# Heads' stage of a hybrid attention and SSD backbone: tensor products in written order, and fewer transfers on the SP queue

## The chip, the cores and the metric

The kernel runs on one core of one Trainium2 chip. The metric is the device time of one execution in microseconds (us). The kernel before takes 2391.28 us, the median of three runs (2390.47 to 2392.25).

## What is computed

Two layers run over 512 latent tokens and 256 context tokens, width 1024, all in float32. The part of a layer that the change touches, cut from the reference:

```python
h  = rmsnorm(x_lat, norm1_w[l]) * (1.0 + sc1) + sh1          # hc the same for context
q, k, v, z, xbc, dtf, dtb = split_proj(h @ w_in)             # 4 heads of 2x64, v 128 wide
q = apply_rope(rmsnorm(q, q_norm_w)); k = apply_rope(rmsnorm(k, k_norm_w))
s = einsum("bqhid,bkhid->bhiqk", q, k_all) * HEAD_DIM ** -0.5
p = softmax(s); w = p[:, :, 0] - lam * p[:, :, 1]            # differential attention
attn = rmsnorm(w @ v_all, subln_w) * (1.0 - lam_init)
ssd  = gated_group_rmsnorm(ssd_bidirectional(...) + d_res * xs, z, ssd_norm_w)
x_lat = x_lat + g1 * (concat([attn, ssd]) @ w_out)
h2 = rmsnorm(x_lat, norm2_w[l]) * (1.0 + sc2) + sh2
x_lat = x_lat + g2 * expert_choice_ffn(h2, ...)              # 16 experts, SwiGLU, top 64 tokens each
```

The context stream is updated in layer 0 only. The vectors `sh`, `sc`, `g` come from `silu(c) @ w_mod`, six blocks of 1024 columns.

## The kernel before

Each layer has four stages: the SSD projections and chunk states, the heads' stage, the output stage, and the experts. Tokens lie in tiles of 128 (four latent, two context). A float32 product is made of three fp32r products (`mm3`, L179): high by high, high by low, low by high part.

In the heads' stage each of four heads projects each of six tiles: `Head.proj` runs eight steps of three products into `pacc` and yields after each step, so a tile has 24 products. Beside these run pieces, each a Python generator: `rope` (norm and rotation, then four transposes `qtr`, L1793), `attend` of the head before (score products `sc` L1828, maximum `nm` L1832, exponentials `e` L1837, weight transposes `wtr` L1855, output products `po` L1860), the last SSD chunks (`yd` L1098, `yo` L1103, `Y` L1139) and the modulation (`macc` L335, from weights `mr` in 512 KB pieces, seven buffers). The score tile `sc` has one buffer in PSUM.

`Slots.tick` advances every piece by one step and draws on the generator of products between them. A tile has two ticks of four steps, so 12 products per tick. The order in which instructions stand on an engine is not the written one: a scheduler orders all engines by its own estimate of when operands are ready, and the engines then run in that fixed order.

In the output stage `op_in` (L1193) loads a tile `mixin` of the concatenated heads, scales it (L1204), transposes it (`mtr`, L1210), and `oacc` products with `w_out` follow; `x_load` brings the residual, and the new `x1` is stored. For layer 0 also the normalised `xn` is stored in `xn2d`, from which the experts gather.

The kernel's loads and stores go through `ld` (L162) and `st` (L169), which issue on the queue of SyncE (SP), in order; a few small loads at the start go through `lds` on GpSimd (POOL). A weight block is loaded as `raw` (four buffers), rounded to its high part on ScalarE (L131) and its low part is made on POOL (L143) or VectorE (L145). The expert weights `gw` are loaded by SP too, in pairs (gate and up, 704 KB each).

Of the kernel before, what the change touches and what calls it, by code (L numbers as in the profile page):

```python
# [18 lines left out]
P = 128  # L19
D = 1024  # L20
# [56 lines left out]
class Slots:  # L77
# [7 lines left out]
    def add(self, *gens):  # L85
        self.live += [[g, None] for g in gens]

    def tick(self, fill=None, n=0, each=0):
        turn, done, first = sorted(self.live, key=lambda x: x[1] is None), 0, True
        while turn:  # L90
            again = []
            for i, x in enumerate(turn):
                x[1] = next(x[0], self)
                if x[1] is STEP:
                    again.append(x)
                while first and not each and done < (n - 1) * (i + 1) // len(turn):
                    next(fill, None)
                    done += 1
            for _ in range(min(each, n - 1 - done)):
                next(fill, None)  # L100
                done += 1
            turn, first = again, False
        while done < n:
            next(fill, None)
            done += 1
        self.live = [x for x in self.live if x[1] is not self]
# [43 lines left out]
class Net:  # L150
# [16 lines left out]

    def st(self, o, i):
        return self.nc.sync.dma_start(o, i)  # L169

    def split(self, hi, lo, x, sub=None):

# [261 lines left out]
    def mixer(self, l):  # L434
        nc, tc, psp = self.nc, self.tc, self.psp
# [10 lines left out]
        q = Slots()  # L446

        if l == 0:
            with tc.manual_schedule(engines=ENGINES):
                mp = open_("mp")  # L450
                self.first(pre)
                f = self.mods_first(pre, mp)
# [70 lines left out]
        first, ssd = [], []  # L523
# [52 lines left out]
        for i, t in enumerate(tiles):  # L576
            f = self.z_proj(l, t, wz, psp, q)
# [13 lines left out]
        self.att1 = open_("at")  # L591
        q.add(self.rope_tables(l, self.att1))
        wo = []
        for h in range(4):
            if h == 1:
                self.attB = open_("atB")
            st = hd[h + 1].stage(W) if h < 3 else None
            hd[h].open()
            for i, t in enumerate(SEQ):
                f = hd[h].proj(t, q)  # L600
                if i == 5 and st:
                    f = paired(f, st)
                for half in range(2):
                    tk = 2 * i + half
                    if ssd and over(ssd):
                        ssd = None
                        zp.release()
                        ch.release()
                        s1.release()
                        com.release()  # L610
                        self.scp.release()
                        self.scp = self.scores(l)
                        mo = open_("mo", "right")
                        mr = lambda: mo.tile([P, 1024], F32, tag="mr", name="mr", bufs=7)
                        q.add(itertools.chain(*([self.mods(0, range(2, 6), mo, mr)] if l == 0 else [self.mods(1, (2, 3, 4), mo, mr)])))
                    if h > 0 and tk in (5, 7, 9, 11):
                        q.add(hd[h - 1].attend(tk // 2 - 2))
                    if l == 0 and h > 0 and tk in (1, 3):
                        q.add(hd[h - 1].attend(NL + tk // 2))
                    q.tick(f, 4)  # L620
                if i % 2:
                    q.add(hd[h].rope(t - 1))
            for _ in st or ():
                pass
        mo.release()
        hp.release()
        self.xnp = open_("xn", "right") if l else None
# [16 lines left out]
        for i, t in enumerate(tiles):  # L644
# [6 lines left out]
            for j in range(nt):  # L651
# [25 lines left out]
                else:  # L677
                    n = 4
# [462 lines left out]
    def z_out(self, l, t, ap):  # L1141

        nc, y = self.nc, self.Y[:, t]
        for g in range(2):
            junk = ap.tile([P, 256], BF16, tag="yj", name="yj", bufs=1)
            nc.scalar.activation(junk, y[:, 256 * g:256 * g + 256], AF.Square, scale=1.0 / 16, accum_out=self.mss[:, t, g:g + 1])
        self.st(self.mixd[l][t * P:(t + 1) * P, 512:1024], y)
        yield


# [32 lines left out]

    def g1_load(self, l, s, op):
        self.G1 = op.tile([P, D], F32, tag="G1", name="G1")
        self.ld(self.G1, self.modd[l, s:s + 1, 2 * D:3 * D].to_broadcast([P, D]))

    def x_load(self, l, t, op):
        self.xs[t] = op.tile([P, D], F32, tag="xr", name="xr", bufs=1)
        self.ld(self.xs[t], self.xsrc(l, t))  # L1190

    def op_in(self, l, t, op, psp):

        nc = self.nc
        mx = op.tile([P, D], F32, tag="mixin", name="mixin", bufs=1)
        n = 4 if t >= NL else 3
        self.ld(mx[:, 512:D], self.mixd[l][t * P:(t + 1) * P, 512:D])
        self.ld(mx[:, 0:n * P], self.mixd[l][t * P:(t + 1) * P, 0:n * P])
        self.mT[t] = mT = [op.tile([P, KD, P], F32, tag=f"mT{j}", name="mT", bufs=2) for j in range(2)]
        rs = yield from self.rsqrt_steps(op, self.mss[:, t, 0:n + 2], n + 2, 1.0, f"mrs{n}")  # L1200
        yield
# [75 lines left out]
    def op_half(self, l, t, b, op, psp):  # L1277
# [14 lines left out]
        if b == 0:  # L1292
            return
        s = int(t >= NL)
        self.st(self.rows_of(l, t), x1)
        yield STEP
        ss = op.tile([P, 1], F32, tag="ss3", name="ss3", bufs=2)
        nc.vector.tensor_tensor(ss, self.ss2[t][:, 0:1], self.ss2[t][:, 1:2], op=OP.add)
# [15 lines left out]
        if l == 0:  # L1314

            xn = self.xn[t]
            nc.vector.tensor_scalar(xn, x1, rs, None, op0=OP.mult)
            self.st(self.xn2d[t * P:(t + 1) * P], xn)
        else:
            nc.vector.tensor_copy(self.rms[:, t:t + 1], rs)  # L1320
        nc.vector.reciprocal(sm, sm)
# [384 lines left out]
class Head:  # L1706
# [107 lines left out]
    def attend(self, t):  # L1814
# [53 lines left out]
        if own:  # L1868
# [4 lines left out]
            nc.tensor.transpose(tr, ob, n.ident)  # L1873
            yield from n.head_split(*([m[:, t] for m in n.oT] if n.oT else [m[:, 3] for m in n.mT[t]]), tr)
            return
        n.st(n.mixd[self.l][t * P:(t + 1) * P, P * self.h:P * self.h + P], ob)


# [41 lines left out]
```

## Time and profile before

| | us |
|---|---|
| median of three runs | 2391.28 |
| the profiled execution | 2389.74 |
| its span in the trace | 2388.0 |
| TensorE (PE) busy | 2176.3 (91%) |
| VectorE (DVE) busy | 931.7 (39%) |
| ScalarE (ACT) busy | 652.2 (27%) |
| GpSimd (POOL) busy | 433.5 (18%) |

The profiled execution is 1.54 us under the median, and 1.74 us of it lie outside the span. A wait is time in which an engine stood still, put down to the instruction that released it last. Products overlap on PE, so the time from one start to the next says what one costs, not its own duration. SPq, ACTq and POOLq are the issuing queues of these engines.

### The profile page before, as it was taken

What the parts mean: (1) busy time and instruction counts of PE and PEld (TensorE: products, weight loads), DVE (VectorE), ACT (ScalarE), POOL (GpSimd) and SP (SyncE); (2) the same over time, 40 slices, a digit from 0 to 9 for tenths busy, and PEclk for the clock granted to TensorE, in tenths of its full rate; (3) what the DMA queues carried; (4) which work ended last, traced back from release to release, by engine and by line L of the source; (5) the groups of instructions that cost most, each with busy time, mean ns of one, the idle gap of its engine ahead of it and who ended that gap; (6) DMA issues with size and microseconds to landing.
All of it is one profiled execution on the core that took longest, in us unless ns stands there. A gap on an engine that the chain in (4) does not pass through costs nothing. (4 is left out here: it accounts for less than half of the span.)

```text
span 2388.0 us, 49731 instructions
## 1 busy us (share of the span) xinstructions
PE 2176.3 (91%) x20620; PEld 1247.0 (52%) x20620; DVE 931.7 (39%) x2586; ACT 652.2 (27%) x1791; POOL 433.5 (18%) x554
## 2 busy tenths in 40 slices
PE   6898998999999999999987988989799999988776
PEld 4677788685444444444435667877543333232322
DVE  5787578772111111111116786786611110101010
ACT  4434477532111111111113334575101010101000
POOL 4464342000101001001003464341000000000000
PEclk9999999999999999999998999999899999999999
DMA  7323723589999999999994226334999999999997
GB/s 250 91 78 102 266 72 107 186 285 344 390 407 401 398 405 393 401 400 400 395 390 127 86 66 198 112 109 139 347 400 416 385 416 410 416 411 415 412 413 314
DMA packets 229790, 701.69 MB, mean 294 GB/s; under 512 B 30340, under 2 KB 79324, under 8 KB 229564
## 3 DMA queue, kind: packets, MB, share of 16 engines
q1 hardware_dynamic: 220076, 681.37, 73.9%
q0 software_dynamic: 9488, 17.14, 3.5%
q8 instruction: 163, 2.67, 0.4%
q14 instruction: 63, 0.52, 0.1%
HBM read 674.66 MB, written 23.76 MB: 292 GB/s over the span
## 5 line engine op out<-in xcount | busy, mean ns | idle before, releaser
L1518 PE MATMUL gl<-gw,xeT 128*32 128x512 f32 (+1 forms) x8192 | 654.8, 466 | 61.9 <-DMA gw<-w_up 59.1
L1518 PEld LDWEIGHTS gl<-gw,xeT 128*32 128x32 f32 x8192 | 279.1, 111 | 441.4 <-issue 396.5
L1559 DVE SCALAR_TENSOR_TENSOR th<-th,gl 128x256 f32<-128x256 f32 (+1 forms) x96 | 37.5, 391 | 698.5 <-ACT th L1558 698.4
L1572 PE MATMUL yl<-rt,hl 128*32 128x512 f32 x2040 | 257.7, 595 | 9.5 <-PE gl L1518 9.2
L1558 ACT ACTIVATE th<-gl 128x256 f32<-128x256 f32 (+1 forms) x96 | 35.1, 366 | 768.1 <-PE gl L1518 761.4
L179 PE MATMUL pacc<-rt,H 128*128 128x384 f32 (+1 forms) x768 | 203.1, 346 | 7.1 <-POOL rt L143 2.4
L1699 DVE SCALAR_TENSOR_TENSOR ys<-yl,gate,G2l 128x512 f32<-128x512 f32 x32 | 24.0, 751 | 380.5 <-PE yl L1572 367.4
L1609 PE MATMUL gc<-gw,xeT 128*32 128x352 f32 x2048 | 171.2, 459 | 0.0
L1700 POOL DMA_INDIRECT out<-ys,sidx x16 | 24.8, 1549 | 730.6 <-DVE ys L1699 589.8
L179 PEld LDWEIGHTS pacc<-rt,H 128*128 128x128 f32 x768 | 134.1, 192 | 19.8 <-issue 6.0
L1572 PEld LDWEIGHTS yl<-rt,hl 128*32 128x32 f32 x2040 | 70.4, 109 | 141.3 <-issue 83.2
L179 PE MATMUL xacc<-H,rt 128*128 128x512 f32 (+1 forms) x448 | 135.9, 381 | 7.0 <-ACT H L816 6.6
L1456 POOL DMA_INDIRECT xe<-xn2d,gidx x16 | 15.1, 943 | 617.6 <-PE xet L1466 507.0
L179 PE MATMUL pacc<-rt,L 128*128 128x384 f32 (+1 forms) x384 | 127.1, 331 | 0.0
L1471 ACT ACTIVATE xeT<-xet,MC,A 128x64 f32<-128x64 f32 (+1 forms) x256 | 74.1, 426 | 178.5 <-PE xet L1466 178.5
L143 POOL TENSOR_TENSOR rt<-raw,rt 128x384 fp32r<-128x384 f32 (+1 forms) x88 | 101.5, 1176 | 80.7 <-ACT rt L131 66.4
L179 PE MATMUL oacc<-woh,mT 128*128 128x512 f32 x304 | 107.4, 411 | 0.0
L1572 PE MATMUL yl<-wd,hl 128*32 128x512 f32 x776 | 102.2, 599 | 2.2 <-DMA wd<-w_down 1.7
L1609 PEld LDWEIGHTS gc<-gw,xeT 128*32 128x32 f32 x2048 | 68.8, 110 | 56.6 <-issue 44.8
L179 PEld LDWEIGHTS xacc<-H,rt 128*128 128x128 f32 x448 | 83.1, 199 | 22.9 <-ACT H L816 7.4
L179 PE MATMUL xacc<-L,rt 128*128 128x512 f32 (+1 forms) x224 | 82.6, 371 | 3.0 <-POOL L L879 2.1
L1485 PE MATMUL xpk<-x,one 128*64 128x512 f32 x256 | 81.8, 633 | 3.4 <-DVE one L1481 3.4
(410 smaller groups left out, 3279.0 us busy)
## 6 DMA issues: line engine op xcount, KB each, us to landing
gw<-w_gate SPq DMA_DIRECT2D x256, 704.0 KB
gw<-w_up SPq DMA_DIRECT2D x256, 704.0 KB
rt<-w_down SPq DMA_DIRECT2D x255, 512.0 KB
wd<-w_down SPq DMA_DIRECT2D x97, 512.0 KB
mr<-w_mod SPq DMA_DIRECT2D x80, 512.0 KB
raw<-w_in SPq DMA_DIRECT2D x48, 256.0 KB
raw<-w_in SPq DMA_DIRECT2D x64, 192.0 KB
RB<-acsd SPq DMA_DIRECT2D x20, 512.0 KB
```

Of the source, the lines that this page charges most:

```text
L143: e.tensor_tensor(lo.bitcast(F32R), x, hi, op=OP.subtract)
L179: self.nc.tensor.matmul(o, a[x].bitcast(F32R), b[y].bitcast(F32R), start=start and i == 0, stop=stop and i == 2, **kw)
L1456: self.nc.gpsimd.indirect_dma_start(out=xe[0:n], out_offset=None, in_=self.xn2d[0:rows], in_offset=bass.IndirectOffsetOnAxis(ap=idx[0:n, e ...
L1471: nc.scalar.activation(xT[:, kk, c:d], tr[:, k, c - a:d - a], AF.Identity, scale=self.A2[:, s, kk:kk + 1], bias=self.MC[:, l, s, 24 + kk:2 ...
L1485: nc.tensor.matmul(ps[64 * j:64 * j + 64], one[:, t], self.x1[t][:, 512 * j:512 * j + 512], start=t == 0, stop=t == NL - 1, skip_group_che ...
L1518: self.nc.tensor.matmul(gl[c][32 * j:32 * j + 32, o:o + n].rearrange("p (u t i) -> p u t i", u=2, i=32), self.xT[:, k, 32 * g:32 * g + 32] ...
L1558: nc.scalar.activation(th, g, AF.Tanh, scale=0.5)
L1559: nc.vector.scalar_tensor_tensor(th, th, 1.0, g, op0=OP.add, op1=OP.mult)
L1572: nc.tensor.matmul(y[64 * j + 32 * g:64 * j + 32 * g + 32], h[:, g, b], wd[b][:, 512 * j:512 * j + 512], start=b == 0, stop=b == NF - 1, s ...
L1609: nc.tensor.matmul(gc[u][32 * j:32 * j + 32].rearrange("p (t i) -> p t i", i=32), xT[:, k, 64:96], w, start=k == 0, stop=k == KD - 1, skip ...
L1699: nc.vector.scalar_tensor_tensor(ys, y, self.gate[:, i, e:e + 1], G2[i], op0=OP.mult, op1=OP.mult)
L1700: nc.gpsimd.indirect_dma_start(out=dst[i], out_offset=bass.IndirectOffsetOnAxis(ap=self.sidx[:, i, e:e + 1], axis=0), in_=ys, in_offset=No ...
```

## The change

`tick` gets an argument `ahead`. With `ahead=2` it draws two steps (six products) first, then advances all pieces without products between them, and then draws the rest (six products). The heads' loop uses it, and stands in a `manual_schedule` of PE: within that loop PE's instructions keep the order in which they are written; the other engines are ordered by the scheduler as before. Stores of `Y`, of `ob` (64 KB each), and of the new residual go to ScalarE's queue (`sta`): 10, 32 and 10 of them. `G1`, the residual loads, the `mixin` loads and the `xn2d` stores go to POOL's queue: 3, 10, 20 and 6 of them.

```diff
-    def tick(self, fill=None, n=0, each=0):
-        turn, done, first = sorted(self.live, key=lambda x: x[1] is None), 0, True
+    def tick(self, fill=None, n=0, each=0, ahead=None):
+        turn, done, first = sorted(self.live, key=lambda x: x[1] is None), 0, ahead is None
+        for done in range(1, 1 + (ahead or 0)):
+            next(fill, None)
         while turn:
...
-            for _ in range(min(each, n - 1 - done)):
+            for _ in range(min(each, n - 1 - done) if ahead is None else 0):
...
+    def sta(self, o, i):
+        return self.nc.scalar.dma_start(o, i)
...
+        heads = tc.manual_schedule(engines={mybir.EngineType.PE})
+        heads.__enter__()
         for h in range(4):
...
-                    q.tick(f, 4)
+                    q.tick(f, 4, ahead=2)
...
+        heads.__exit__(None, None, None)
...
-        self.st(self.mixd[l][t * P:(t + 1) * P, 512:1024], y)
+        self.sta(self.mixd[l][t * P:(t + 1) * P, 512:1024], y)
...
-        self.ld(self.G1, self.modd[l, s:s + 1, 2 * D:3 * D].to_broadcast([P, D]))
+        self.lds(self.G1, self.modd[l, s:s + 1, 2 * D:3 * D].to_broadcast([P, D]))
...
-        self.ld(self.xs[t], self.xsrc(l, t))
+        self.lds(self.xs[t], self.xsrc(l, t))
...
-        self.ld(mx[:, 512:D], self.mixd[l][t * P:(t + 1) * P, 512:D])
-        self.ld(mx[:, 0:n * P], self.mixd[l][t * P:(t + 1) * P, 0:n * P])
+        self.lds(mx[:, 512:D], self.mixd[l][t * P:(t + 1) * P, 512:D])
+        self.lds(mx[:, 0:n * P], self.mixd[l][t * P:(t + 1) * P, 0:n * P])
...
-        self.st(self.rows_of(l, t), x1)
+        self.sta(self.rows_of(l, t), x1)
...
-            self.st(self.xn2d[t * P:(t + 1) * P], xn)
+            self.lds(self.xn2d[t * P:(t + 1) * P], xn)
...
-        n.st(n.mixd[self.l][t * P:(t + 1) * P, P * self.h:P * self.h + P], ob)
+        n.sta(n.mixd[self.l][t * P:(t + 1) * P, P * self.h:P * self.h + P], ob)
```

From the first to the last `pacc` product, PE's listing has 151 runs of one kind in layer 0 before and 117 after, of which 71 and 41 are `pacc`; in layer 1 it has 104 and 87, of which 50 and 32. The 576 products per layer are the same.

On PE, at the start of layer 0's heads' stage, where the last SSD chunks are still running; before:

```order
L179 MATMUL zacc<-rt,L 128x512
L1098 MATMUL yd<-XS,G 128x64 x4
L1103 MATMUL yo<-H,Cc 128x512
L179 MATMUL pacc<-rt,H 128x384 x2
L179 MATMUL pacc<-rt,L 128x384
```

and after:

```order
L186 MATMUL zacc<-rt,L 128x512
L186 MATMUL pacc<-rt,H 128x384 x2
L186 MATMUL pacc<-rt,L 128x384
L186 MATMUL pacc<-rt,H 128x384 x2
L186 MATMUL pacc<-rt,L 128x384
L1108 MATMUL yd<-XS,G 128x64 x4
L1113 MATMUL yo<-H,Cc 128x512
```

Six `pacc` products moved ahead of the SSD products `yd`.

On PE, in the second head of layer 0, from a modulation piece to the first score product; before:

```order
L330 MATMUL macc<-bmod,ident 32x256 x4
L335 MATMUL macc<-mr,sC 32x256 x16
L1855 MATMUL wtr<-ident,e_2858 128x128 x2
L179 MATMUL pacc<-rt,H 128x384 x2
L179 MATMUL pacc<-rt,L 128x384
L1793 MATMUL qtr<-ident,rope 128x128 x4
L179 MATMUL pacc<-rt,H 128x384 x2
L179 MATMUL pacc<-rt,L 128x384
L1828 MATMUL sc<-KK,Q 128x512
```

and after:

```order
L337 MATMUL macc<-bmod,ident 32x256 x4
L342 MATMUL macc<-mr,sC 32x256 x16
L1865 MATMUL wtr<-ident,e_2857 128x128 x2
L1803 MATMUL qtr<-ident,rope 128x128 x4
L1838 MATMUL sc<-KK,Q 128x512
```

The two threes of products between the pieces have gone to the six on either side of the pieces.

On SP, in the last two heads of layer 0 (`ob` is a tile of attention output, `raw` a block of weights); before:

```order
L169 DMA mixd<-ob 128x128
L169 DMA modd<-mrow 4x256 x2
L169 DMA mixd<-ob 128x128 x5
L162 DMA raw<-w_in 128x3x128 x4
L162 DMA raw<-w_out 128x512 x4
L169 DMA mixd<-ob 128x128 x6
L162 DMA raw<-w_out 128x512 x4
```

and after:

```order
L165 DMA raw<-w_in 128x3x128
L172 DMA modd<-mrow 4x256 x2
L165 DMA raw<-w_in 128x3x128 x4
L165 DMA raw<-w_out 128x512 x10
L165 DMA mr<-w_mod 128x1024
```

The stores of `ob` are gone from between the loads; on ScalarE each stands behind the two instructions that make it, and often just ahead of the exponentials `e` of the next tile.

## Rows read from the trace of the kernel before

**Rows 1.** By stretch: length, busy us of PE, PEld, DVE, ACT, POOL; PE clock.

```profile
206.50:397.30 190.80, 179.81 (x1263) 158.23 (x1262) 130.04 (x356) 114.14 (x332) 73.63 (x114) 0.98 0.42 138
397.30:412.50 15.20, 8.16 (x46) 7.31 (x45) 13.69 (x51) 10.34 (x28) 5.75 (x8) 0.66 0.70 226
...
1440.80:1598.00 157.20, 151.33 (x1110) 136.06 (x1109) 112.86 (x306) 88.53 (x252) 60.85 (x99) 0.98 0.40 128
```

**Rows 2.** Waits of PE from 206.5 to 397.3 us (total, times, longest).

```profile
PE yd L1098 <- DVE G L1091: 3.5, 1, 3.5
PE sc L1828 <- ACT e L1837: 2.7, 3, 1.3
PE pacc L179 <- DVE Y L1139: 2.4, 1, 2.4
PE pacc L179 <- POOL rt L143: 1.8, 4, 1.0
PE pacc L179 <- ACT rt L131: 0.7, 1, 0.7
```

**Rows 3.** Waits of PE from 1430 to 1598 us.

```profile
PE yd L1098 <- DVE G L1091: 5.9, 2, 5.2
PE sc L1828 <- ACT e L1837: 1.0, 2, 0.7
PE pacc L179 <- POOL qss L1725: 1.0, 1, 1.0
...
PE pacc L179 <- POOL rt L143: 0.7, 2, 0.4
PE pacc L179 <- ACT rt L131: 0.6, 1, 0.6
```

**Rows 4.** PE in time order: start, duration, line, work, count.

```profile
287.12 0.60 PE L179 MATMUL pacc<-rt,H 128*128 128x384 f32 x2
...
287.73 0.51 PE L179 MATMUL pacc<-rt,H 128*128 128x384 f32 x2
...
288.26 0.52 PE L179 MATMUL pacc<-rt,H 128*128 128x384 f32 x2
```

**Rows 5.** PE in time order, starts of the two heads' stages and a `macc` piece.

```profile
221.60 1.01 PE L179 MATMUL pacc<-rt,H 128*128 128x384 f32 x2 [2.37 <-DVE Y L1139]
...
1443.32 0.40 PE L179 MATMUL pacc<-rt,H 128*128 128x256 f32 x2
...
1443.67 0.40 PE L179 MATMUL pacc<-rt,H 128*128 128x256 f32 x2
...
1466.05 1.93 PE L335 MATMUL macc<-mr,sC 128*32 128x256 f32 x32
```

**Rows 6.** SP's queue in time order; a duration spans the whole group.

```profile
317.97 28.22 SPq L169 DMA_DIRECT2D mixd<-ob  x5
349.01 4.71 SPq L162 DMA_DIRECT2D raw<-w_in  x4
...
565.44 0.45 SPq L162 DMA_DIRECT2D gw<-w_up  x1
574.89 0.33 SPq L162 DMA_DIRECT2D gw<-w_gate  x1
...
1467.13 2.59 SPq L162 DMA_DIRECT2D raw<-w_in  x4
```

**Rows 7.** Waits of ACT from 206.5 to 412 us.

```profile
ACT e L1837 <- DVE nm L1833: 14.4, 12, 3.0
...
ACT rt L131 <- DMA raw<-w_in: 2.5, 5, 0.7
```

**Rows 8.** ACT in time order: a tile `mixin` is scaled.

```profile
475.79 0.71 ACT L1204 ACTIVATE mixin<-mixin,mrs_y 128x128 f32<-128x128 f32 x2
```

**Rows 9.** PE in time order: the transposes of that tile.

```profile
486.09 0.93 PE L1210 MATMUL mtr<-ident,mixin 128*128 128x128 f32 x7
```

**Rows 10.** Waits of PE from 545 to 1300 us, layer 0's experts.

```profile
PE gl L1518 <- DMA gw<-w_up: 16.4, 10, 2.5
```

## The prediction

> **What bounds the kernel now.** I read the busy shares first: TensorE (PE) works 2176 of 2388 us, no other engine half of the span, so time is won only where PE stands still or spends time on its own order. Then the table by stretch, for the part that the change touches. In the heads' stage PE is busy 179.81 of 190.80 us in layer 0 and 151.33 of 157.20 in layer 1 [rows 1]. All idle time there is 11.0 and 5.9 us; that caps what removed waits can give. In the transition to the output stage another engine sets the pace: VectorE is busy 13.69 of 15.20 us, PE 8.16 [rows 1].
>
> The lists of PE's waits say what the idle time is. In layer 0: 3.5 us for the SSD's `G`, 2.4 for `Y`, 2.7 for the exponentials `e`, 2.5 for weight blocks `rt` from POOL and ACT [rows 2]. In layer 1: 5.9 for `G`, 1.0 for `e`, 2.3 around weight blocks and the memset `qss` in POOL's way [rows 3]. None of them is a store.
>
> **Order on PE.** The timeline shows what a change of kind costs. Behind `po` the first three products take from 287.12 to 287.73, 0.61 us; the next three from 287.73 to 288.26, 0.53 [rows 4]. I take 0.09 us per switch, between this 0.08 and 0.10 for the pairs that start a longer run elsewhere. Layer 0 has 151 − 117 = 34 runs fewer, layer 1 104 − 87 = 17: −3.1 and −1.5 us. This lies on PE's own path. Nearest bounds: nothing, where such a place waits anyway, and 0.2 us per run, or −10 together.
>
> **The start.** Six products now stand ahead of `yd`, inside its wait. In layer 0 that gives nothing: the second tile waits for `Y` until 221.60 anyway, and `Y` follows from `yd`, `yo` and VectorE, which do not move [rows 5]. The 2.4 us for `Y` grow by what the first wait loses. In layer 1 no such wait stands there. Three of its narrower products take 1443.67 − 1443.32 = 0.35 us, six take 0.7 [rows 5]. Half of the second `yd` stood behind 24 products; all of it now stands behind 42, so its wait, 5.9 − 5.2 = 0.7 us [rows 3], goes too. Together −1.4 us; bounds 0 (a wait for `Y` appears as in layer 0) and −2.5 (the clock, low after a wait, has a shorter one to recover from).
>
> **Score products against exponentials.** The score tile has one buffer, so the next `sc` waits for both `e` of the one before. Between two `sc` lie 24 `pacc` products, `wtr` and `po`, in both kernels: before spread unevenly, from 21 to 27, now always 24. `sc` stands right behind `wtr`, with nothing between. Where it already waits, five times [rows 2, 3], a faster PE only waits longer: two saved switches each, 5 × 0.18 = 0.9 us of the gain are lost; with some new places I take +1.0. Bounds: −3.7, all of these waits gone by even spacing, and +5, a further 0.2 us at each of some 25 attends.
>
> **Weight blocks.** The stall that SP shows is real: five stores of `ob` hold it from 317.97 for 28 us, and `raw` follows only at 349.01 [rows 6]. But ACT stood only 2.5 us for `raw` in all, in pieces of at most 0.7 [rows 7]. Of the `rt` waits in layer 1 the blocks loaded at 1467.13 are the cause [rows 6], and SP reached them behind eight `mr` loads with seven buffers, the eighth of which needs the `macc` of 1466.05 [rows 5]. That piece moves six products later in the order, so these blocks come no sooner. In layer 0 POOL's own instructions release most of it, 1.8 us in four waits [rows 2], and not a load. I put 0; bounds −4.8 (2.5 + 2.3, all gone) and +2.
>
> **Stores on ACT.** 42 stores of `Y` and `ob` and 10 of the residual now take ACT's time; an issue takes 0.33 to 0.45 us on SP's queue [rows 6], and I assume the same. A store often stands just ahead of `e`, which waits for VectorE's `nm` 14.4 us in 12 times, a mean of 1.2 us [rows 7]: the issue fits in there. Hence 0; bounds 0 and 25 × 0.45 = +11, if each of some 25 in the two heads' stages delayed `e` and PE behind it.
>
> **Loads on POOL.** A `mixin` tile is the first that would be missed. ACT has scaled one by 475.79 + 0.71 = 476.50; PE transposes it at 486.09 [rows 8, 9], 9.6 us later. A load that lands some us later is hidden; I take 0, bounds 0 and +5 for both output stages. POOL issues before them only gathers and weight parts, and is 39% busy in the heads' stage (73.63 of 190.80).
>
> The Trainium skill, "SBUF — State Buffer", section "SBUF: two separate sides", speaks against this move: descriptors of a DMA issued by GpSimd cannot be written while VectorE runs an instruction in a two-port mode, so the transfer starts only behind it. No row here shows a plain load on POOL. By that rule each `mixin` load is later by one VectorE instruction; by the rows the 9.6 us take this up, and the sum stays.
>
> **Earlier expert weights.** SP without waits can issue `gw` sooner. At 565.44 it has issued all it has buffers for and issues the next at 574.89 [rows 6], after PE has used one. So the buffers are full before PE asks, and an earlier start fills them only earlier: 0, with −16 as the far bound, all of layer 0's waits for `gw` [rows 10].
>
> The transition I leave as it is: VectorE's instructions there are the same, in slightly another order.
>
> **Sum.** −3.1 − 1.5 − 1.4 + 1.0 = −5.0 us. What is won on PE before the experts starts their first product so much earlier, and their buffers free up so much earlier, so I carry it to the end in full. The profiled execution took 2389.74, which gives 2384.7; against the median of 2391.28 it gives **2386.3 us**.
>
> **Rivals.** *The waits take it back* (no change). The heads' stage is paced by the chain `sc`, `nm`, `e`, and PE's fewer switches turn into longer waits. For it: VectorE is busy 130 and ACT 114 of 190.8 us, and three waits for `e` already stand there. Against it: these are only 3.7 us in all. Only the start would remain, −1.4: 2389.9 us.
>
> *ScalarE's queue becomes the wait* (slower). A store on ACT that must wait for an older transfer holds the exponentials and copies behind it. Place: `ob` stores next to the `mr` loads, in the first half of the heads' stage. It decides when a store takes longer than the mean 1.2 us that `e` waits for `nm`. With 0.45 us lost at each of 25 stores, +11 against −5.0: 2397 us. For it: ACT has its queue to itself now and an issue blocks all behind it; against it: on SP the queue waited for `ob`, not for room.
>
> *The weight stream comes earlier* (faster by more). If half of the 16.4 us of waits for `gw` [rows 10] went, the time would be 2391.28 − 5.0 − 8.2 = 2378.1. For it: the output stage leaves much of the DMA unused in places. Against it: the full buffers at 565.44.
>
> *The order is the gain*: if even spacing also removes the 3.7 us for `e` and the 4.8 us for weight blocks, −5.0 − 1.0 − 3.7 − 4.8 = −14.5, 2376.8 us. It shares its chance with the one before.
>
> **Chances.** The forecast, −2 to −9 us, 0.48; waits take it back 0.20; ScalarE's queue 0.18; the two larger gains 0.14 together. What can be told from no change is about 0.2%, 4.8 us, so my forecast lies on that edge. Of its 0.48 I count 0.32 as faster and 0.16 as the same. Faster 0.32 + 0.14 = 0.46; same 0.16 + 0.18 + 0.02 = 0.36; slower 0.02 + 0.16 = 0.18. The range, 2375 to 2398, takes in the larger gains and most of ScalarE's case; the forecast's own is 2382 to 2389.
>
> **What would show it.** Right: in the heads' stages PE's busy time falls by some 3 and 1.5 us with the same products, the wait of 0.7 us in layer 1 is gone, the wait for `Y` in layer 0 is longer, and the waits for `e` are somewhat more. The first `gw` is issued earlier, and the gap before the next one after the buffers are full is longer. Wrong: waits of `e` or `wT` behind a store on ACT; PE waiting for `mtr` behind `mixin`; weight-block waits that are gone; or a layer 0 expert stage that is shorter, not only earlier.

## The result and the profile after

The changed kernel takes 2410.28 us, the median of five runs (2404.81 to 2414.73); the kernel before took 2390.47 on the same chip (2388.07 to 2392.25). The ratio is 1.0076, with a 95% interval of [1.006, 1.0092]: slower by some 18 us, where 2386.3 was forecast, and outside the range of 2375 to 2398. The profiled execution has a span of 2408.5 us, 20.5 more than before.

By stretch of the profiled execution, in us; the bounds are the starts of TensorE's last `zacc`, last `pacc`, first `oacc`, first `gl` and last `gl` product of each layer. The four columns on the right are experiments that are told below (e1: the order alone; e4: loads on GpSimd alone; e25 and e27: two more edits):

| stretch | before | after | e1 order alone | e4 loads alone | e25 | e27 |
|---|---|---|---|---|---|---|
| start to end of `zacc`, layer 0 | 206.8 | 208.0 | 207.4 | 203.0 | 205.4 | 207.5 |
| heads (to the last `pacc`), layer 0 | 190.4 | 192.8 | 190.2 | 189.2 | 189.3 | 193.6 |
| transition (to the first `oacc`) | 15.4 | 21.0 | 18.3 | 18.7 | 16.0 | 20.9 |
| output stage (to the first `gl`) | 133.1 | 138.9 | 131.6 | 140.7 | 128.9 | 133.3 |
| experts, layer 0 | 703.6 | 699.2 | 702.3 | 701.9 | 705.2 | 703.8 |
| projections, layer 1 | 183.2 | 187.4 | 185.5 | 185.1 | 183.0 | 183.2 |
| heads, layer 1 | 165.5 | 167.4 | 168.8 | 165.8 | 166.6 | 168.2 |
| transition, layer 1 | 14.6 | 19.0 | 16.9 | 18.4 | 15.6 | 19.4 |
| output stage, layer 1 | 116.7 | 121.8 | 115.9 | 123.3 | 121.1 | 116.9 |
| experts, layer 1 | 635.5 | 632.8 | 636.1 | 635.5 | 629.1 | 629.3 |
| rest | 23.2 | 20.2 | 23.5 | 20.9 | 20.1 | 21.0 |
| span | 2388.0 | 2408.5 | 2396.5 | 2402.5 | 2380.3 | 2397.1 |

So the heads' stages, for which the order was written, lost 4.3 us together, the two transitions 10.0, and the two output stages, which the order does not touch, 10.9. Only the experts gave something back, 7.1; the other lines make up the remaining 2.4. Each column is one execution: the first line, which no edit touches, goes from 203.0 (e4, e8) to 209.3 us (e15), so a difference of a few us in one line counts only where a wait or other runs support it.

The same stretches in the view by windows, after (columns as in [rows 1]; the third line is layer 0's output stage):

```profile
208.00:400.80 192.80, 179.09 (x1261) 159.83 (x1260) 127.90 (x355) 111.50 (x323) 73.88 (x113) 0.96 0.42 137
400.80:421.80 21.00, 9.07 (x48) 7.63 (x48) 16.14 (x54) 14.11 (x37) 10.56 (x15) 0.67 0.70 245
421.80:560.70 138.90, 132.96 (x799) 103.69 (x797) 93.36 (x370) 55.73 (x154) 15.72 (x26) 0.93 0.60 212
1447.30:1614.70 167.40, 156.05 (x1120) 140.69 (x1118) 119.95 (x320) 93.22 (x263) 69.99 (x108) 0.96 0.41 129
```

PE is as busy for as many products in layer 0's heads as before, 179.09 against 179.81 [rows 1], and idle longer, 13.7 against 11.0 us. The clock that the throttle granted is lower in both heads' stages, 0.96 where it was 0.98 in layer 0 and 0.97 in layer 1 (over 1432.5 to 1598.0), and in layer 0's output stage 0.93 where it was 0.96. The last line is 10 us longer than the one in [rows 1] mostly because `pacc` now starts right behind `zacc`, 8 us earlier in the stage.

PE's waits in layer 0's heads, after; the columns are those of [rows 2]:

```profile
PE pacc L186 <- POOL rt L146: 6.6, 5, 5.0
PE pacc L186 <- DVE Y L1149: 3.8, 1, 3.8
PE sc L1838 <- ACT e L1847: 2.1, 3, 1.1
PE yd L1108 <- DVE G L1101: 0.8, 1, 0.8
PE pacc L186 <- ACT rt L134: 0.5, 1, 0.5
```

and in layer 1, against [rows 3]:

```profile
PE yd L1108 <- DVE G L1101: 4.6, 1, 4.6
PE pacc L186 <- POOL rt L146: 3.3, 3, 1.3
PE sc L1838 <- ACT e L1847: 1.8, 3, 1.1
PE pacc L186 <- ACT rt L134: 1.2, 1, 1.2
```

The start went as forecast: the wait for `G` fell from 3.5 to 0.8 us in layer 0 and from 5.9 in two to 4.6 in one in layer 1, and that for `Y` grew from 2.4 to 3.8. But the waits for weight blocks `rt` grew, from 2.5 to 7.1 us in layer 0 and from 1.3 to 4.5 in layer 1. The longest is one wait of 5 us.

**The wait for a weight block.** It stands at the second head's first tile. After, PE and POOL in order of time:

```profile
255.76 0.44 PE L186 MATMUL pacc<-rt,H 128*128 128x384 f32 x1 [0.46 <-ACT rt L134]
...
259.40 0.76 POOL L1796 TENSOR_TENSOR rope<-rope,qrs_y 128x128 f32<-128x128 f32 x2 [2.67 <-DVE qrs_y L230]
260.12 3.87 POOL L146 TENSOR_TENSOR rt<-raw,rt 128x384 fp32r<-128x384 f32 x4
261.16 0.69 PE L186 MATMUL pacc<-rt,H 128*128 128x384 f32 x1 [4.96 <-POOL rt L146]
...
263.21 0.56 PE L1838 MATMUL sc<-KK,Q 128*128 128x256 f32 x1
```

and the same place before, which no row above shows:

```profile
254.33 0.36 PE L1828 MATMUL sc<-KK,Q 128*128 128x256 f32 x1
...
255.54 1.93 PE L335 MATMUL macc<-mr,sC 128*32 128x256 f32 x32
...
258.36 0.76 POOL L1786 TENSOR_TENSOR rope<-rope,qrs_y 128x128 f32<-128x128 f32 x2 [3.11 <-DVE qrs_y L223]
259.08 4.08 POOL L143 TENSOR_TENSOR rt<-raw,rt 128x384 fp32r<-128x384 f32 x4
...
260.13 0.44 PE L179 MATMUL pacc<-rt,H 128*128 128x384 f32 x1 [1.01 <-POOL rt L143]
```

In both kernels POOL makes `rt` late, because the `rope` ahead of it in its queue waits about 3 us for VectorE. Before, PE spent that time on `sc` and `macc`; in the written order these stand behind the product that waits, at 263.21 and later. Counted from the last `zacc`, POOL begins the block 52.1 us later, before 52.3: the weight did not come later. The work that had covered for it did.

**The late `mixin`.** In the output stage of layer 0, after:

```profile
494.42 1.07 POOL L169 DMA_DIRECT2D mixin<-mixd  x2 [3.14 <-PE mtr L1220]
494.99 0.33 SPq L165 DMA_DIRECT2D gw<-w_gate  x1
...
499.84 0.91 ACT L1214 ACTIVATE mixin<-mixin,mrs_y 128x256 f32<-128x256 f32 x2 [4.53 <-DMA mixin<-mixd]
...
503.11 0.17 DVE L213 TENSOR_SCALAR mrs_y<-mrs_m 128x6 int32<-128x6 int32 x1 [2.57 <-ACT mixin L1214]
505.30 0.67 DVE L1257 TENSOR_TENSOR x<-x,xr 128x512 f32<-128x512 f32 x1
506.03 0.66 PE L1298 MATMUL xtr<-ident,x 128*128 128x128 f32 x4 [2.61 <-DVE x L1257]
```

The load is issued at 494.42 and ScalarE gets it at 499.84, 5.4 us later. VectorE's `mrs_y` for the next tile writes the small buffer that ScalarE still reads for this one, so it waits; the sum `x` stands behind it in VectorE's queue; and PE waits for `x`. The windows around that wait (same columns, PE's busy time first, granted clock third from the end):

```profile
498.00:502.00 4.00, 4.00 (x20) 3.29 (x19) 2.04 (x7) 2.16 (x6) 0.00 (x0) 1.00 1.02 413
502.00:506.00 4.00, 1.42 (x7) 0.82 (x5) 2.89 (x12) 1.08 (x4) 0.00 (x0) 1.00 1.01 420
506.00:510.00 4.00, 3.97 (x17) 3.54 (x18) 4.00 (x25) 1.28 (x3) 0.54 (x1) 0.61 1.01 418
510.00:514.00 4.00, 4.00 (x15) 3.47 (x14) 1.44 (x10) 0.00 (x0) 0.00 (x0) 0.50 1.02 420
514.00:518.00 4.00, 4.00 (x17) 3.44 (x16) 1.78 (x5) 1.27 (x2) 1.07 (x2) 0.61 0.17 69
518.00:522.00 4.00, 4.00 (x21) 3.31 (x20) 3.88 (x18) 1.33 (x5) 0.54 (x1) 1.00 0.65 252
```

After a wait of 2.6 us PE runs for some 12 us at 0.61, 0.50 and 0.61 of full clock, about the lower level of 1.2 GHz: 12 × (1 − 0.57) = 5 us lost, twice the wait itself. Before, the load came from SP at the like place, three lines in order of time:

```profile
487.05 0.79 SPq L162 DMA_DIRECT2D mixin<-mixd  x2
487.90 0.42 SPq L162 DMA_DIRECT2D gw<-w_gate  x1
...
489.67 0.91 ACT L1204 ACTIVATE mixin<-mixin,mrs_y 128x256 f32<-128x256 f32 x2 [1.45 <-DMA mixin<-mixd]
```

It took 2.6 us. The loads of expert weights `gw` stand *behind* `mixin` in that queue, and were held back while it waited for its buffer. The DMA engines were 0.57 busy from its issue to 489.67; after, 0.98 from 494.42 to 499.84, and 1.02 in the 3.4 us before.

### The profile page after: what moved, and what is told of

It reads as the page before. It is cut to its first block, busy times and chain, and to the rows that moved or that the text cites. A ratio compares the mean times of both kernels' runs of the same rounds, so it can differ in the third digit from the quotient of the medians.

```text
span 2408.5 us, 49715 instructions
## 1 busy us (share of the span) xinstructions
PE 2185.2 (91%) x20620; PEld 1254.6 (52%) x20620; DVE 934.5 (39%) x2586; ACT 653.5 (27%) x1791; POOL 457.6 (19%) x593
## 5 line engine op out<-in xcount | busy, mean ns | idle before, releaser
L1528 PE MATMUL gl<-gw,xeT 128*32 128x192 f32 (+1 forms) x8192 | 650.8, 464 | 60.1 <-DMA gw<-w_up 59.2
L186 PE MATMUL pacc<-rt,H 128*128 128x384 f32 (+1 forms) x768 | 202.5, 345 | 15.8 <-POOL rt L146 9.9
L186 PEld LDWEIGHTS pacc<-rt,H 128*128 128x128 f32 x768 | 139.6, 195 | 26.4 <-POOL rt L146 13.2
```

The source lines that it names most:

```text
L186: self.nc.tensor.matmul(o, a[x].bitcast(F32R), b[y].bitcast(F32R), start=start and i == 0, stop=stop and i == 2, **kw)
L1528: self.nc.tensor.matmul(gl[c][32 * j:32 * j + 32, o:o + n].rearrange("p (u t i) -> p u t i", u=2, i=32), self.xT[:, k, 32 * g:32 * g + 32] ...
```

## The experiments

All times are medians in us, with the ratio to the kernel before on the same chip and its 95% interval. None changes what is computed.

**One part at a time: e1, e2, e3, e4.** e1 has only the written order and the new tick, with every transfer on SP; e2 only the moved transfers; e3 only the stores on ScalarE; e4 only the loads and `xn2d` on GpSimd.

```diff
 e1: heads.__enter__() ... q.tick(f, 4, ahead=2) ... heads.__exit__(None, None, None)
 e3: self.sta(mixd, y);  n.sta(mixd, ob);  self.sta(self.rows_of(l, t), x1)
 e4: self.lds(self.G1, ...);  self.lds(self.xs[t], ...);  self.lds(mx, ...);  self.lds(xn2d, xn)
 e2: e3 and e4
```

Expected of e1: 

> The written order on PE alone (six products, all pieces, six products); every load and store on SP as before. Theory 1 (the loads on POOL cost the time: late mixin tiles, ScalarE blocked behind them): about before, 2386 to 2392 us, since the order's own switches give 3 to 5 us and its new waits take a part. Rival, theory 2 (the order costs it: waits for weight blocks and scores): 2400 to 2410 us, with the wait for rt of about 5 us near 261 us and the wait for mixin in the transition still there.

Expected of e2: 

> The queue moves alone (stores on ScalarE, loads and xn2d on POOL); PE ordered by the scheduler and products spread as before. Theory 1: most of the loss, 2400 to 2410 us, with ScalarE waiting 4 us and more for a mixin load in the output stage. Theory 2 (the order): 2386 to 2393 us.

Expected of e3: 

> Only the stores of Y, ob and the residual on ScalarE's queue, nothing else changed. Theory 1: within 3 us of before, 2388 to 2393 us, since an issue takes 0.33 us and ScalarE has idle time. Rival, theory 3 (stores block ScalarE): 2398 us or more, with exponentials late behind stores.

Expected of e4: 

> Only G1, residual loads, mixin loads and xn2d stores on POOL's queue, nothing else changed. Theory 1: 2400 us or more, the output stages of both layers longer by some 5 us each. If POOL's queue alone is harmless and the loss needs SP's earlier weight loads beside it (theory 4: contention with expert weights): 2388 to 2394 us.

Measured: e1 2398.15, 1.0033 [1.0021, 1.0044]; e2 2399.83, 1.0039 [1.0027, 1.0051]; e3 2391.57, 0.9998 [0.9988, 1.0008]; e4 2404.22, 1.0071 [1.0053, 1.009]. The order and the moved transfers each cost, and add up to the whole (0.33% and 0.39% against 0.76%). e3 and e4 did as theory 1 has it; e1 fell between its two theories and e2 just under the range of theory 1, since each part carries about half. The stores cost nothing alone. The loads alone cost more than with the stores beside them; why, no run tells.

**Which load: e7, e8.** Of the moved loads, only `mixin` (e7), and only the others (e8).

```diff
 e7: self.lds(mx[:, 512:D], ...);  self.lds(mx[:, 0:n * P], ...)
 e8: self.lds(self.G1, ...);  self.lds(self.xs[t], ...);  self.lds(xn2d, xn)
```

Expected of e7: 

> Only the mixin loads on POOL's queue; residual loads, G1, xn2d and all stores on SP. Theory 1a (a late mixin tile stops ScalarE, then VectorE's next mrs_y, then PE, and PE's clock falls): most of what the four moved kinds cost together (+13.5 us), 2398 to 2405 us, with a PE wait for x in layer 0's output stage. Rival 1b (the other loads and stores, xn2d before the gather above all): 2389 to 2394 us.

Expected of e8: 

> The complement: G1, residual loads and xn2d stores on POOL's queue, mixin loads on SP. Theory 1a: 2389 to 2394 us. Rival 1b: 2398 us or more.

Measured: e7 2400.72, 1.0036 [1.0024, 1.0048]; e8 2397.32, 1.0024 [1.001, 1.0037]. e7 did as theory 1a has it; e8 fell between its two. `mixin` is the larger part by the medians, but not all; how `G1`, `xr` and `xn2d` cost their share stays open. e7 has the chain of the changed kernel with nothing else moved:

```profile
493.40 0.91 ACT L1211 ACTIVATE mixin<-mixin,mrs_y 128x256 f32<-128x256 f32 x2 [5.53 <-DMA mixin<-mixd]
...
497.87 0.17 DVE L213 TENSOR_SCALAR mrs_y<-mrs_m 128x6 int32<-128x6 int32 x1 [4.78 <-ACT mixin L1211]
...
500.78 1.12 PE L1295 MATMUL xtr<-ident,x 128*128 128x128 f32 x4 [4.83 <-DVE x L1254]
```

**Where the order costs: e14, e15, e20.** The written order and the new tick in heads 2 and 3 alone (e14), in head 2 alone (e15), in all but head 1 (e20); the rest is left to the scheduler and the tick of before, and all transfers are on SP.

```diff
+            heads = tc.manual_schedule(engines={mybir.EngineType.PE}) if h > 1 else None   # e14
+            heads = tc.manual_schedule(engines={mybir.EngineType.PE}) if h == 2 else None  # e15
+            heads = tc.manual_schedule(engines={mybir.EngineType.PE}) if h != 1 else None  # e20
```

Expected of e14: 

> Written order on PE and six-pieces-six ticks in the last two heads only; first two heads as before; all loads and stores on SP. Theory 2a (the order loses in the first heads, where PE stands 5 us for weight blocks with ready macc and sc products behind): 2389 to 2394 us, rt waits as before. Theory 2b (it loses at the end, in the transition, where wtr waits 3.3 us for QL): 2395 to 2399 us, that wait still there.

Expected of e15: 

> Written order and six-pieces-six ticks in the third head only, so that neither the start nor the end of the heads' stage changes. 12 and 6 switches less than before: if only start and end lose, 2388 to 2390 us, 1 to 2 us under before (0.09 us a switch). If the order costs something in every head: 2393 us or more.

Expected of e20: 

> The new order of TensorE (source order, two products ahead of the pieces) in heads 0, 2 and 3 of both layers; head 1 is left to the scheduler; all transfers on SP. With all four heads in source order it was 2398.2 us, 7.4 over before; with heads 2 and 3 alone 2393.3. Theory (the weight block that comes late to head 1's first tile, 4.96 us of waiting for GpSimd's rt in layer 0 and 3 to 4 in layer 1, with the pieces behind the waiting product in written order): 2393 to 2395 us, and the wait on rt before head 1's first products back at about 2 us in layer 0. Rival (head 0 and the start of the projections carry the loss): 2396 to 2398 us.

Measured: e14 2393.27, 1.0007 [0.9999, 1.0016]; e15 2391.13, 1.0001 [0.9992, 1.0009]; e20 2392.76, 1.001 [1.0001, 1.002]. With head 1 back under the scheduler, about two thirds of the loss of e1 are gone, and the longest wait on POOL's `rt` in layer 0's heads is 1.0 us where e1 has 5.0. So most of the order's loss comes with head 1; e14 did as theory 2a has it, and e20 came 0.2 us under its theory's range. By stretch the difference between e1 and e20 stands in layer 1's heads (168.8 and 165.4 us). In layer 0 they are alike (190.2 and 189.8, before 190.4): there shorter waits for `G` (0.8 us for 3.5), `Y` (1.6 for 2.4) and `e` (1.9 for 2.7) paid for e1's wait of 5.0. e15, a head without late weight blocks, came between its two theories and shows no gain from fewer switches.

**Order or bunching: e10, e11.** e10 has the new tick and leaves PE to the scheduler; e11 has the written order with the tick of before.

```diff
 e10: q.tick(f, 4, ahead=2)
 e11: heads.__enter__() ... q.tick(f, 4) ... heads.__exit__(None, None, None)
```

Expected of e10: 

> Only the tick's shape: two steps of the products are drawn ahead of all pieces and the rest behind them, as in the change, but the scheduler still orders TensorE; all transfers on SP. Theory (the loss of the order comes from a fixed queue in which ready pieces stand behind a waiting product): 2389 to 2393 us, since the scheduler can still put a ready piece ahead. Rival (the bunching of the pieces itself is at fault): 2396 to 2399 us, as with the order.

Expected of e11: 

> Source order on TensorE in all four heads, but with the tick of before: pieces spread one by one among the steps of the products, nothing drawn ahead; all transfers on SP. Theory (a fixed order sets ready pieces behind a product that waits for its weight block, whatever the spacing): a wait on GpSimd's rt of 3 to 5 us at head 1's first tile in layer 0, and 2395 to 2399 us. Rival (the bunching costs, as it did with the scheduler free, and the source order alone is cheap): 2390 to 2393 us and no rt wait over 2 us.

Measured: e10 2397.08, 1.0027 [1.0016, 1.0039]; e11 2398.02, 1.0028 [1.0016, 1.004]. e11 did as the theory has it: a wait on `rt` of 3.1 us and the loss, without bunching. e10 did as the rival has it: the loss without the wait (its longest on `rt` is 1.2 us). So bunching has a price of its own. The two stand at different places. e11's is in the heads' stages (196.2 and 167.8 us for 190.4 and 165.5), with the transitions as before (15.6 and 14.6). e10's is behind them: its heads' stages are 190.0 and 164.8, its transitions 18.2 and 16.5 for 15.4 and 14.6, and layer 1's output stage 119.6 for 116.7; that execution was 3.5 us faster than e10's median. The longer transitions go with the new tick in the last head. The four runs of the order that have it there (e1, e10, e14, e20) show 17.4 to 18.3 and 16.5 to 16.9 us; e11 and e15, which do not, 15.6 and 15.8, and 14.6 and 14.3. In the four, PE's transposes `wtr` wait 3.3 us for ScalarE in each transition; in the two, and before, at most 0.2. In layer 0 ScalarE's casts to `Q`, which stood ahead of the last `pacc` product (397.25), now stand behind it (397.65 in e1) and ahead of what `wtr` waits for. Before:

```profile
395.38 1.50 ACT L1804 CAST Q<-qtr 64x256 fp32r<-64x256 f32 x4
399.53 0.41 PE L1855 MATMUL wtr<-ident,e 128*128 128x128 f32 x2 [0.18 <-DVE QL L1810]
```

and in e1:

```profile
398.99 1.50 ACT L1814 CAST Q<-qtr 64x256 fp32r<-64x256 f32 x4
403.43 0.69 PE L1865 MATMUL wtr<-ident,e 128*128 128x128 f32 x2 [3.26 <-ACT ob L1874]
```

That chain is read from the traces; the place is shown by which runs have it. The two prices do not add, since e1 has both and cost 1.0033: with the new tick the start gains what e11 does not (e11 still waits 3.5 us for `G`).

**The shared small buffer: e16, e21.** e16 is e7 with VectorE's small tiles `mrs` given their own buffers for odd and even tiles; e21 is the kernel before with the same edit.

```diff
-        rs = yield from self.rsqrt_steps(..., f"mrs{n}")
+        rs = yield from self.rsqrt_steps(..., f"mrs{n}{t % 2}")
```

Expected of e16: 

> mixin on GpSimd's queue as in the run that moved mixin alone (2400.7 us, 8.6 over before), and one edit more: the five small tiles mrs_m, mrs_y, mrs_h, mrs_e, mrs_q of a tile's scale get their own buffers for odd and even tiles, so that VectorE's mrs_y for the next tile no longer waits until ScalarE has read the old one while scaling a late mixin. Theory (the price of a late mixin is paid through VectorE's queue: ScalarE's scaling 5.5 us late, mrs_y 4.8, the sum x behind it, TensorE's xtr 4.8, then about 8 us at a low granted clock): the xtr wait of 4.8 us and the low clock behind it go in layer 0, layer 1 keeps its share, so the time falls to 2393 to 2396 us. Rival (the late mixin costs through its own transposes and through ScalarE's queue, the shared tile is only what the records name): the time stays within 2 us of 2400.

Expected of e21: 

> The kernel before, all transfers on SP and the scheduler's order, with the five small mrs tiles in own buffers for odd and even tiles. Theory: before, ScalarE's wait for mixin is only about 1.5 us and little is behind it, so the time stays within 1 us of 2391. Rival: the shared tile costs in the kernel before as well, and the time falls by 2 to 4 us, a version faster than both kernels.

Measured: e16 2395.53, 1.0015 [1.0006, 1.0024]; e21 2390.03, 1.0001 [0.9992, 1.001]. In e16 `mixin` is as late as in e7, and PE no longer waits for `xtr`:

```profile
494.10 0.91 ACT L1211 ACTIVATE mixin<-mixin,mrs_y 128x256 f32<-128x256 f32 x2 [5.89 <-DMA mixin<-mixd]
...
496.30 0.66 PE L1295 MATMUL xtr<-ident,x 128*128 128x128 f32 x4
```

That takes 0.21% off, 5 us, as its theory has it, while e21 shows no gain without the late load: the chain through VectorE's queue is shown, and it is a little over half of what the move of `mixin` cost.

**Both repairs in the whole change: e24.** Head 1 to the scheduler and the old tick, and own buffers for `mrs`.

Expected of e24: 

> The whole change with two repairs: head 1 is left to the scheduler and the old tick, and the five small mrs tiles have own buffers for odd and even tiles. The change was 2410.3 us, 0.76% over before. Theory (the two causes add): the first repair took 5.4 us off the order alone, the second 5.2 off mixin alone, so 2398 to 2402 us, a ratio of 1.003 to 1.0045. Rival (in the whole change other waits are late next and take the repairs back): over 2405 us.

Measured: 2408.22, 1.007 [1.0055, 1.0085]. The rival was right: two edits that took some 5 us each where they stood alone took 2 off the whole, which the intervals do not tell from nothing. The trace shows what came next, in order of time:

```profile
516.56 1.49 ACT L1216 ACTIVATE mixin<-mixin,mrs_y 128x256 f32<-128x256 f32 x4 [6.41 <-DMA mixin<-mixd]
518.89 0.16 DVE L1333 RECIPROCAL rsm<-rsm 128x1 f32<-128x1 f32 x1 [4.14 <-ACT rex L1325]
...
519.28 0.36 PE L1387 MATMUL tap<-ident,tavx 16*64 16x16 f32 x2 [4.20 <-DVE tavx L1354]
```

ScalarE waits 4.8 us for the `mixin` scaled at 500.26, which now costs PE nothing, and 6.4 for the next; behind that one on its queue stand the router's exponentials `rex`; VectorE waits for these, and PE for VectorE. Relieving a victim does not help while the late load stays. So the question became why it is late.

**Why `mixin` is late: e17, e25, e26.** e17 puts `mixin` on ScalarE's queue; e25 puts on GpSimd's queue both `mixin` and, behind it, the `gw` loads of each layer's first expert; e26 moves only these `gw` loads.

```diff
 e17: self.sta(mx[:, 512:D], ...);  self.sta(mx[:, 0:n * P], ...)
 e25: self.lds(mx, ...)  and  (self.ld if e else self.lds)(w[:, 0], I["w_gate"] ...)   # and w_up
 e26:                         (self.ld if e else self.lds)(w[:, 0], I["w_gate"] ...)   # and w_up
```

Expected of e17: 

> Only the mixin loads move, off SP onto ScalarE's queue instead of GpSimd's. Theory (the load lost its place ahead of the expert weights gw in SP's queue: without the waiting mixin in front, SP issues the gw loads of 704 KB as soon as their buffers are free, and mixin's 448 KB share the DMA engines with them): a mixin wait of 4 to 6 us on ScalarE in layer 0 as on GpSimd's queue, and 2396 to 2402 us. Rival (GpSimd's issue itself is slow): mixin lands within 3 us of its issue, and 2389 to 2393 us.

Expected of e25: 

> Mixin and the gw loads of the first expert of each layer are both on GpSimd's queue, so that gw stands behind mixin in one queue again, as on SP before. Theory: mixin lands within 3.5 us of its issue, the wait of 5.5 us on ScalarE goes, and the time is 2390 to 2394 us. Rival (GpSimd's issue is what makes mixin late): a wait of 4 us or more stays and 2397 to 2402 us.

Expected of e26: 

> The kernel before with one move: the gw loads of the first expert of each layer (16 issues a layer) go to GpSimd's queue; mixin and all else stay on SP. Theory (it is the order between mixin and gw): mixin, though on SP, meets the gw traffic and ScalarE waits over 3 us for it in one or more tiles of layer 0, 2394 to 2400 us. Rival (what counts is only the queue that mixin itself is issued on): ScalarE's waits for mixin stay at 2.2 us and less, 2389 to 2393 us.

Measured: e25 2382.08, 0.9947 [0.9933, 0.9961]; e17 2387.66, 0.9981 [0.9972, 0.9991]; e26 2385.54, 0.9973 [0.996, 0.9985]. All three are faster than the kernel before, e25 by more than its theory had.

e25, where `gw` follows `mixin` on POOL:

```profile
485.54 1.07 POOL L169 DMA_DIRECT2D mixin<-mixd  x2 [15.95 <-ACT mT L1220]
486.66 0.54 POOL L169 DMA_DIRECT2D gw<-w_gate  x1
...
488.41 0.91 ACT L1211 ACTIVATE mixin<-mixin,mrs_y 128x256 f32<-128x256 f32 x2 [2.18 <-DMA mixin<-mixd]
```

2.9 us from issue to use, with the DMA engines 0.53 busy (485.5 to 488.5), against 6.2 us and 1.00 in e7 (487.2 to 493.4), for the same load on the same queue. So POOL's issue is not what made it slow; `gw` in its way was. The Trainium skill, "Trainium Kernel Development and Optimization", section "Key Constraints", says that transfers issued from the three queues run on the same 16 DMA engines and interleave, so that issuing from several saves only issue time; these two runs agree.

e17 and e26 missed. In e17 `mixin` does meet the traffic, with waits of 2.5 and 2.1 us on ScalarE for one tile of layer 0 and 4.5 for one of layer 1, but in layer 0 no such PE wait came of it: beside two that the kernel before has as well (`sc` 3.9 us for 4.7, `mtr` 3.4 for 2.2, both where the stage starts), PE's longest there is 0.9 us. In e26's layer 0 `mixin` was issued at 484.11 and the next `gw` at 485.43, so it kept its place, and ScalarE waited 2.4 us. In its layer 1 eight `gw` loads went out on POOL in the 5 us ahead of the load that SP issued:

```profile
1660.31 0.81 SPq L165 DMA_DIRECT2D mixin<-mixd  x2
...
1667.64 0.91 ACT L1211 ACTIVATE mixin<-mixin,mrs_y 128x256 f32<-128x256 f32 x2 [6.19 <-DMA mixin<-mixd]
```

That is 7.3 us with the DMA engines 1.01 busy, where the same load took 2.7 us and 0.54 before. So `mixin` is late on SP's queue as well when `gw` is ahead of it on another, which is against e26's rival. Both are faster than before all the same. Where e25 and e26 win is seen only by stretch: layer 0's output stage is 128.9 and 128.7 us for 133.1, layer 1's experts are 629.1 and 629.3 for 635.5. Why is not tested.

**The whole change with `gw` behind `mixin`: e27.** The changed kernel with the edit of e26.

Expected of e27: 

> The whole change with one edit: the gw loads of the first expert of each layer (16 issues a layer) go to GpSimd's queue, where they stand behind the mixin loads, as they stood behind them on SP before. Theory (the larger part of the loss is that gw overtakes mixin): the same edit took 18.6 us off the kernel in which mixin alone had moved (2400.7 to 2382.1 us), so at least 10 of them come off the change: 2391 to 2400 us, and ScalarE's wait for mixin near 500 us falls from 4.5 to under 3 us. Rival (in the whole change other waits are late next and take it back, as with the two repairs before): over 2405 us.

Measured: 2402.1, 1.0053 [1.004, 1.0066]. That is 8.2 us off by the medians, 0.23% by the ratios; less than the 10 that the theory had at least, more than its rival. The same edit takes 7.1 us off the kernel before (e26), so the time does not show what the late load cost in the whole change. The trace shows that it is gone at its place in layer 0:

```profile
497.63 0.91 ACT L1214 ACTIVATE mixin<-mixin,mrs_y 128x256 f32<-128x256 f32 x2 [2.02 <-DMA mixin<-mixd]
```

with the clock at full from 496 to 516 us, where the changed kernel had its slow windows from 506 to 518; two of them:

```profile
500.00:504.00 4.00, 3.96 (x19) 2.94 (x18) 3.99 (x16) 1.01 (x4) 0.01 (x1) 1.00 1.02 412
504.00:508.00 4.00, 4.00 (x29) 3.62 (x28) 4.00 (x26) 1.07 (x3) 2.09 (x4) 1.00 0.99 355
```

The output stages are 133.3 and 116.9 us again, as before the change (133.1 and 116.7). For layer 1 that is no proof: e25 has 121.1 us there with its last load on time (a wait of 2.3 us), e17 116.4 with a wait of 4.5, so what lengthened that stage stays open. By stretch the heads' stages (193.6 and 168.2) stay 5.9 us longer than before and the transitions (20.9 and 19.4) 10.3, while layer 1's experts are 6.2 shorter.

## Why the prediction was wrong

**Weight blocks, put at 0 with bounds −4.8 and +2: the step that failed first.** It asked whether the blocks come sooner, and answered rightly that they do not. It did not ask what PE does while they are late. The row of 1.8 us in four waits [rows 2] was what remained of a wait that `sc` and `macc` covered, and the written order took that cover away. These waits grew by 7.8 us in the two layers together; shorter waits for `G` paid for a part, so that the two stages grew by 4.3. e20 shows the place, e11 the mechanism.

**Loads on POOL, put at 0 with bounds 0 and +5: the step that failed by most.** The 9.6 us between the scaling of `mixin` and its transposes [rows 8, 9] were read as slack for the load. They are slack for PE's transposes only. Behind ScalarE's scaling stand copies, and behind a shared buffer stands VectorE's sum, which PE needs next. The step weighed how long an issue on POOL takes; it left out what `mixin` had been moved past, the `gw` loads that SP's wait had held back. Measured alone, the loads cost 0.71%, some 17 us (e4), beside the stores 0.39%, some 9 us (e2), and `mixin` alone 0.36% (e7). e16 shows the chain, e7 against e25 and e26's layer 1 the cause of the lateness, and e27's trace that the wait goes in the whole change too. The share of `G1`, `xr` and `xn2d` (0.24%, e8) and the 5.1 us of layer 1's output stage stay open. That PE would wait for `mtr` behind `mixin` was named as what would show the step wrong; it came in the transition (6.3 us for 2.2 in layer 0, of which e1 has 3.3 by the order alone), while in the output stage the wait was for `xtr`.

**The price of a wait.** All terms counted a wait at its length. In the output stage one of 2.6 us brought some 5 us more at the lower clock.

**The transition, left as it is: the third step that failed.** It grew by 5.6 and 4.4 us, by 2.9 and 2.3 with the order alone and by 3.3 and 3.8 with the loads alone, as the table shows. The step counted VectorE's instructions as the same; it did not ask which of the pieces' work would fall behind the last product. In the changed kernel ScalarE is busy 14.11 us there for 10.34 and VectorE 16.14 for 13.69 [rows 1], and the order's part comes with the new tick in the last head (e10, e14, against e11, e15). PE also waits there 6.3 us for `mixin` on ScalarE, which has a cast of `w_out` ahead of it that waited 5.1 us for its load. That second chain was read and not tried by a run of its own.

**Order on PE, −4.6.** Not seen. The sign that was named, PE's busy time lower by some 3 and 1.5 us, did not come: over the bounds of the table it is 0.3 lower in layer 0 (179.09 for 179.41) and 1.6 higher in layer 1 (156.05 for 154.44), at the lower clock. Head 2 alone in written order saves 12 and 6 switches and would have won some 1.6 us; the interval of e15, −1.9 to +2.2 us, does not exclude that. e10's loss says that bunching has a price which the term did not hold. The cap of 5.9 us on layer 1's idle time was read over a stretch that begins behind the wait for `G`; over the whole stage it was 11.1 (165.50 less 154.44). No term of the sum hung on it.

**The start, −1.4, and score products, +1.0.** The start was right in the main: in layer 1 the waits for `G` fell by 1.3 us; in layer 0 that for `Y` took back 1.4 of 2.7, where all was expected to go. The waits for `e` went from 3.7 to 3.9 us, less than counted.

**Stores on ACT, 0.** Right (e3), and with it the rival "ScalarE's queue becomes the wait" is wrong. It had the sign of the result by a mechanism that played no part.

**Earlier expert weights, 0.** Taken as harmless since the buffers are full in time. They were also the rival of other loads for the DMA engines; the sum had no term for that. Layer 0's expert stage did get shorter, by 4.4 us, which the prediction named as a sign that it was wrong; but e3, whose loads are as before, has 700.4 us there as well, so one execution does not settle it.

## What to carry to other kernels

When a load leaves an in-order queue, ask what it was holding back there: a wait in a queue can be what keeps bulk traffic behind a small urgent load, and then the two belong in one queue (e7 against e25; e26's layer 1). A short wait in the table of waits may be a long one that other work covers, so before an order is fixed, list what runs during each late operand, and what work will stand behind the last product of the stage. And look for slack behind every instruction that is queued after the waiting one, on its engine and on those that share its buffers, not only at the operand's own reader.

## What the runs showed of the hardware

- A wait of PE of 2.6 us, after a stretch at full clock, was followed by windows at 0.61, 0.50 and 0.61 of it; in e27, without that wait, the same stretch ran at 1.00.
- A plain load issued by POOL was used 2.9 us after its issue (e25), one by SP 2.6 us (before); with the DMA engines full it took 6.2 on POOL (e7) and 7.3 on SP (e26, layer 1). Late is not yet costly: in the kernel before, SP's load of 512.18 took 6.4 us with the engines 0.99 busy, and PE did not wait. POOL spent mostly 0.53 to 0.6 us on an issue, SP mostly 0.33 to 0.45. The Trainium skill, "SBUF — State Buffer", section "SBUF: two separate sides", has descriptors of GpSimd's DMAs wait for VectorE's two-port instructions; the 0.3 us between 2.9 and 2.6 leave room for little of that here.
- Two repairs worth some 5 us each alone took 2 off the whole, inside the noise (e24): behind a load that is still late, the wait moved to the next instruction in ScalarE's queue.
